# A split-precision MLP: one 512-column product under each high part of the weights, and a VectorE add of its two halves

## Chip, cores, metric

One core of one Trainium2 chip. The metric is device time in microseconds (us), the median of several executions.

## What is computed

Two decoder blocks of two layers each, on 256 rows of 1024 columns in float32: latent attention, an MLP, block attention with a relative bias, a second MLP, then a gated delta rule and a second attention. The change touches the two MLPs only. Cut to them, the reference is:

```python
def sq_relu_mlp(h, w_in, w_out):
    a = jax.nn.relu(h @ w_in)
    return (a * a) @ w_out
...
        h = rms_norm(x, mlp_norm[i])
        x = x + sq_relu_mlp(h, mlp_w_in[i], mlp_w_out[i])
```

`w_in` is 1024 x 4096, `w_out` 4096 x 1024, for each of the two layers.

## The kernel before

**Split products.** Every float32 operand is held as two fp32r tiles, a high part (a copy rounded to fp32r, made on ScalarE) and a low part (the rest, a subtraction on VectorE). A product of split operands is three matmuls (`mm3`): high by high, high by low, low by high.

**Weights.** `load_w` moves 128 x 1024 float32 by one DMA of SyncE's queue into a `raw` tile (four buffers), then writes the high part (line 166, ScalarE) and the low part (line 167, VectorE; for f = 0 GpSimd). `w_in` blocks go to tiles `whi` and `wlo` (four buffers each), `w_out` blocks to fixed slots, printed as `s` in the trace.

**The MLP** (`mlp`). `transpose_x` writes the normed rows' transpose `hT`: for each k of 8 a high part and a low part of 128 x 256, in two slots. Then a loop over 16 blocks f of 256 hidden columns:

- the first product: for each half j of 128 hidden columns and each k of 8, `mm3` with the weights as the stationary operand and `hT` as the moving one (256 columns), 48 matmuls into one PSUM tile `p` with both halves side by side (for f = 0 into two tiles);
- Relu out of PSUM into `r` (line 671; line 664 for f = 0), the square `sq` (line 673), its high part `ah` (line 676) and low part `al` (line 677);
- the split of two `w_out` blocks;
- in layer 0 a piece of the bias setup (`extra`): masks on VectorE (line 402), four matmuls (line 418) into two PSUM tiles, two copies on ScalarE (line 420);
- the second product of the block before (`second(f - 1)`), 24 matmuls of 512 columns, with `ah` and `al` as the stationary operand, added up over all f in four PSUM tiles `acc`.

PSUM has four `acc` and four `aux` buffers; `p`, the tiles of line 418 and those of the transposes take `aux`. `r`, `sq`, `ah` and `al` take `w2k` tiles (seven buffers).

**Order.** Each engine takes its own queue in the order written when the kernel is built. A planner makes that order from the program's; it isn't the program's order: in the trace the high part of `w_in` block f + 2 stands ahead of the Relu of f on ScalarE.

Of the kernel before, what the change touches and what calls it, by code (L numbers as in the profile page):

```python
# [11 lines left out]
F32R = mybir.dt.float32r  # L12
I32 = mybir.dt.int32
AF = mybir.ActivationFunctionType
ALU = mybir.AluOpType
# [4 lines left out]
P = 128  # L20
S = 256
NT = 2
D = 1024
KD = D // P
# [86 lines left out]
def kernel(ctx: ExitStack, tc: tile.TileContext, I: dict, out: bass.AP, small_at: dict):  # L111
    nc = tc.nc
    V, A, G, T = nc.vector, nc.scalar, nc.gpsimd, nc.tensor
# [10 lines left out]
    def slot(i, shape, dt=F32):  # L124

        return big.tile(shape, dt, tag=f"s{i}", name=f"s{i}")

    def w2k(shape, dt=F32):
        return wk.tile(shape, dt, tag="w2k", name="w2k", bufs=7)
# [4 lines left out]
    def acc_tile():  # L134
        return ps.tile([P, 512], F32, tag="acc", name="acc")

    def aux_tile():
        return ps.tile([P, 512], F32, tag="aux", name="aux")
# [34 lines left out]
    def mm3(o, l, r, start, stop):  # L173
        T.matmul(o, lhsT=l[0], rhs=r[0], start=start, stop=False)  # L174
        T.matmul(o, lhsT=l[0], rhs=r[1], start=False, stop=False)  # L175
        T.matmul(o, lhsT=l[1], rhs=r[0], start=False, stop=stop)  # L176

    def sl(pair, *idx):
        return (pair[0][idx], pair[1][idx])
# [32 lines left out]
    ident, cmask = C["ident"], C["cmask"]  # L212
    xT0 = slot(10, [P, KD, S])
    x = cp.tile([P, NT, D], F32, tag="x", name="x")

    def gain(name, k=0):
        return C[name][:, k:k + 1]
# [24 lines left out]
    def ms_eps(src, name, after=None):  # L242

        ss = st.tile([P, NT, 2], F32, tag="ss", name="ss")
        with queued(after):
            for t in range(NT):
                mean_sq(ss, src, t)
        e = st.tile([P, NT], F32, tag="mse" + name, name="mse")
        V.tensor_tensor(e, ss[:, :, 0], ss[:, :, 1], op=ALU.add)
        V.tensor_scalar(e, e, 1.0 / D, EPS, op0=ALU.mult, op1=ALU.add)  # L250
        return e

    def evac_split(hi, lo, p, g=None):

        if g is None:
            i = A.activation(hi, p, AF.Copy)
            j = V.tensor_tensor(lo, p, hi.bitcast(F32), op=ALU.subtract)
        else:
            i = A.activation(hi, p, AF.Copy, scale=g)  # L259
            j = V.scalar_tensor_tensor(lo, p, g, hi.bitcast(F32), op0=ALU.mult, op1=ALU.subtract)  # L260
        return i.ins, j.ins

    def pair_tile(i, n):
        return slot(i, [P, n, S], F32R), slot(i + 1, [P, n, S], F32R)

    def transpose_x(src, gnames, slots):

        outs = [pair_tile(tg, KD) for tg in slots]
        for k2 in range(KD // 2):
            p = aux_tile()  # L270
            for j in range(2):
                k = 2 * k2 + j
                for t in range(NT):
                    T.transpose(p[:, j * 256 + t * P:j * 256 + (t + 1) * P], src[:, t, k * P:(k + 1) * P], ident)
            for j in range(2):
                k = 2 * k2 + j
                for (hi, lo), (gn, off) in zip(outs, gnames):
                    last = evac_split(hi[:, k], lo[:, k], p[:, j * 256:(j + 1) * 256], gain(gn, off + k))
        return outs, last

    def wview(name, l=None):
        w = I[name] if l is None else I[name][l]
        return w.rearrange("(k p) n -> p k n", p=P)
# [349 lines left out]


    def mlp(l, extra=None):
        (hT,), last = transpose_x(x, [("mlp_norm", 8 * l)], [1])
        r2 = st.tile([P, NT], F32, tag="r2", name="r2")
        w1 = wview("mlp_w_in", l)
        w2 = wview("mlp_w_out", l)
        ya = [[acc_tile() for _ in range(2)] for _ in range(NT)]  # L640
        NF = DFF // 256
        pend = []

        def second(f, aa, wc):
            for kk in range(2):
                for hf in range(2):
                    for t in range(NT):
                        mm3(ya[t][hf], sl(aa, slice(None), kk, slice(t * P, (t + 1) * P)),
                            sl(wc[kk], slice(None), slice(hf * 512, (hf + 1) * 512)),
                            f == 0 and kk == 0, f == NF - 1 and kk == 1)  # L650

        for f in range(NF):
            wc = load_w(w1[:, :, f * 256:(f + 1) * 256], KD, 256, (G,) if f == 0 else None, after=last if f == 1 else None)
            r = w2k([P, 512])
            if f == 0:

                pj = [aux_tile() for _ in range(2)]
                for k4 in range(2):
                    for j in range(2):
                        for k in range(4 * k4, 4 * k4 + 4):  # L660
                            mm3(pj[j][:, 0:S], sl(wc[k], slice(None), slice(j * P, (j + 1) * P)), sl(hT, slice(None), k),
                                k == 0, k == KD - 1)
                for j in range(2):
                    A.activation(r[:, j * S:(j + 1) * S], pj[j][:, 0:S], AF.Relu)
            else:
                p = aux_tile()
                for j in range(2):
                    for k in range(KD):
                        mm3(p[:, j * S:(j + 1) * S], sl(wc[k], slice(None), slice(j * P, (j + 1) * P)),
                            sl(hT, slice(None), k), k == 0, k == KD - 1)  # L670
                A.activation(r, p, AF.Relu)
            sq = w2k([P, 512])
            V.tensor_tensor(sq, r, r, op=ALU.mult)
            ah = w2k([P, 2, S], F32R)
            al = w2k([P, 2, S], F32R)
            A.activation(ah.rearrange("p a b -> p (a b)"), sq, AF.Copy)  # L676
            V.tensor_tensor(al.rearrange("p a b -> p (a b)"), sq, ah.rearrange("p a b -> p (a b)").bitcast(F32),  # L677
                            op=ALU.subtract)
            wo = load_w(w2[:, 2 * f:2 * f + 2, :], 2, D, (G,) if f == 0 else None,
                        [slot(i, [P, 2048], F32R) for i in ((5, 6), (7, 11))[f % 2]],  # L680
                        last if f == 0 else None)
            pend.append((f, (ah, al), wo))
            if f == 3:
                V.reciprocal(r2, ms_eps(x, "m", last))
            if extra is not None:
                extra(f)
            if len(pend) > 1:
                second(*pend.pop(0))
        second(*pend.pop(0))
        for hf in range(2):  # L690
            for t in range(NT):
                xs = x[:, t, hf * 512:(hf + 1) * 512]
                V.scalar_tensor_tensor(xs, ya[t][hf], r2[:, t:t + 1], xs, op0=ALU.mult, op1=ALU.add)
# [626 lines left out]
```

## Time and profile before

| | us |
|---|---|
| median of 3 runs (lowest, highest) | 964.49 (960.13, 966.01) |
| profiled execution | 965.93 |
| its span, first to last instruction | 964.1 |

| engine | busy us | share of the span |
|---|---|---|
| TensorE, matmuls | 905.0 | 94% |
| TensorE, weight loads | 789.9 | 82% |
| VectorE | 635.4 | 66% |
| ScalarE | 522.7 | 54% |
| GpSimd | 151.1 | 16% |

Weight loads overlap matmuls, and the ends of matmuls are modelled: for what a matmul costs in a stream, take the distance from one start to the next, not its duration. PE is TensorE's matmuls, PEld its weight loads, DVE VectorE, ACT ScalarE, POOL GpSimd, SP SyncE; SPq is SyncE's queue, where loads are issued. A wait names the instruction that released it.

### The profile page before, as it was taken

The numbers are of one execution on the slowest core, as the hardware profiler recorded it, in microseconds if no ns is written. First come the engines' busy times: TensorE is split into PE (matmuls) and PEld (weight loads), VectorE is DVE, ScalarE is ACT, GpSimd is POOL, SyncE is SP. The second block draws the span as 40 slices with busy tenths as digits, with TensorE's granted clock in tenths as the row PEclk, the third lists the DMA queues.
The fourth block names the chain that finished last, engine by engine and source line by source line (L and its number), as shares of the span: only waits on it lengthen the run. The fifth ranks groups of instructions, "written<-read, shape, count | busy, mean of one in ns | idle before, by whom it ended". The sixth has DMA issues, their size and how long they took to land. (4 is left out here: it accounts for less than half of the span.)

```text
span 964.1 us, 14699 instructions
## 1 busy us (share of the span) xinstructions
PE 905.0 (94%) x5474; PEld 789.9 (82%) x5474; DVE 635.4 (66%) x1335; ACT 522.7 (54%) x967; POOL 151.1 (16%) x194
## 2 busy tenths in 40 slices
PE   8799889999999999999999999998995998998995
PEld 8676589989998878778999999888994986887784
DVE  6897376655556666757554555678983688757775
ACT  6576354644556556646534454478653136754652
POOL 1421122222222300022000000010387000000000
PEclk9799999999999999999999999999997999999998
DMA  8345247677767864436666566354843115445431
GB/s 292 115 146 186 66 131 220 192 198 214 205 197 209 166 196 151 154 109 198 196 195 198 175 195 183 105 166 140 215 149 98 45 41 181 135 170 174 133 109 67
DMA packets 97304, 154.62 MB, mean 160 GB/s; under 512 B 10840, under 2 KB 65920, under 8 KB 96976
## 3 DMA queue, kind: packets, MB, share of 16 engines
q1 hardware_dynamic: 87072, 141.53, 46.9%
q0 software_dynamic: 10016, 12.11, 6.0%
q8 instruction: 43, 0.70, 0.3%
q14 instruction: 29, 0.24, 0.1%
q10 hardware_dynamic: 144, 0.03, 0.0%
HBM read 147.84 MB, written 5.78 MB: 159 GB/s over the span
## 5 line engine op out<-in xcount | busy, mean ns | idle before, releaser
L167 DVE TENSOR_TENSOR wlo<-raw,whi 128x1024 fp32r<-128x1024 f32 (+3 forms) x194 | 236.7, 1223 | 201.9 <-ACT whi L166 200.6
L166 ACT ACTIVATE whi<-raw 128x1024 fp32r<-128x1024 f32 (+3 forms) x202 | 206.0, 1025 | 217.0 <-DMA raw<-in_mlp_w_in_dram 137.6
L174 PE MATMUL acc<-whi,s 128*128 128x512 f32 (+2 forms) x408 | 162.1, 401 | 3.5 <-ACT whi L166 2.6
L175 PE MATMUL acc<-wlo,s 128*128 128x512 f32 (+2 forms) x408 | 160.4, 394 | 0.5 <-DVE wlo L167 0.5
L176 PE MATMUL acc<-whi,s 128*128 128x512 f32 (+2 forms) x408 | 158.9, 391 | 0.0
L176 PE MATMUL aux<-s,wlo 128*128 128x256 f32 (+2 forms) x528 | 149.5, 283 | 3.1 <-DVE wlo L167 3.1
L174 PE MATMUL aux<-s,whi 128*128 128x256 f32 (+2 forms) x528 | 149.4, 283 | 2.3 <-DVE s L260 2.3
L175 PE MATMUL aux<-s,whi 128*128 128x256 f32 (+2 forms) x528 | 149.3, 283 | 0.0
L174 PEld LDWEIGHTS aux<-s,whi 128*128 128x128 f32 (+2 forms) x528 | 99.6, 189 | 4.6 <-DVE s L260 2.8
L176 PEld LDWEIGHTS aux<-s,wlo 128*128 128x128 f32 (+2 forms) x528 | 99.6, 189 | 3.9 <-DVE wlo L167 3.6
L174 PE MATMUL acc<-s,w2k 128*128 128x512 f32 x256 | 100.1, 391 | 1.7 <-ACT w2k L676 1.7
L176 PE MATMUL acc<-s,w2k 128*128 128x512 f32 x256 | 100.2, 391 | 1.1 <-DVE w2k L677 1.1
L175 PEld LDWEIGHTS aux<-s,whi 128*128 128x128 f32 (+2 forms) x528 | 99.6, 189 | 1.6
L175 PE MATMUL acc<-s,w2k 128*128 128x512 f32 x256 | 100.0, 391 | 0.0
L174 PEld LDWEIGHTS acc<-whi,s 128*128 128x128 f32 x408 | 77.6, 191 | 20.6 <-ACT whi L166 3.1
L176 PEld LDWEIGHTS acc<-whi,s 128*128 128x128 f32 x408 | 78.6, 193 | 14.0 <-DVE s L1278 0.3
L175 PEld LDWEIGHTS acc<-wlo,s 128*128 128x128 f32 x408 | 78.2, 192 | 13.2 <-DVE wlo L167 1.3
L167 DVE TENSOR_TENSOR s<-raw,s 128x1024 fp32r<-128x1024 f32 x64 | 75.7, 1219 | 5.3 <-ACT s L166 5.3
L176 PE MATMUL acc<-s,wlo 128*128 128x256 f32 x256 | 73.4, 288 | 6.2 <-DVE wlo L167 6.2
L175 PE MATMUL acc<-s,whi 128*128 128x256 f32 x256 | 73.7, 288 | 0.5 <-DVE s L260 0.2
L174 PE MATMUL acc<-s,whi 128*128 128x256 f32 x256 | 73.7, 288 | 0.4 <-ACT s L259 0.2
L166 ACT ACTIVATE s<-raw 128x1024 fp32r<-128x1024 f32 x68 | 68.3, 1048 | 7.2 <-DMA raw<-in_mlp_w_out_dram 6.0
(357 smaller groups left out, 1486.2 us busy)
## 6 DMA issues: line engine op xcount, KB each, us to landing
raw<-in_mlp_w_in_dram SPq DMA_DIRECT2D x64, 512.0 KB, 5.3
raw<-in_mlp_w_out_dram SPq DMA_DIRECT2D x64, 512.0 KB, 3.9
raw<-in_gdn_w_in_dram SPq DMA_DIRECT2D x32, 512.0 KB, 4.4
raw<-in_moba_w_qkv_dram SPq DMA_DIRECT2D x24, 512.0 KB, 4.4
raw<-in_fox_w_in_dram SPq DMA_DIRECT2D x16, 512.0 KB, 4.9
raw<-in_kv_w_dram SPq DMA_DIRECT2D x16, 512.0 KB, 3.9
raw<-in_mla_w_o_dram SPq DMA_DIRECT2D x8, 512.0 KB, 3.9
bias_d<-s POOLq DMA_DIRECT2D x64, 64.0 KB, 4.5
```

Of the source, the lines that this page charges most:

```text
L166: i = A.activation(hi[:, :k * b], rs, AF.Copy)
L167: j = e.tensor_tensor(lo[:, :k * b], rs, hi[:, :k * b].bitcast(F32), op=ALU.subtract)
L174: T.matmul(o, lhsT=l[0], rhs=r[0], start=start, stop=False)
L175: T.matmul(o, lhsT=l[0], rhs=r[1], start=False, stop=False)
L176: T.matmul(o, lhsT=l[1], rhs=r[0], start=False, stop=stop)
```

## The change

`transpose_x2` stores `hT` so that for each k the high and the low part stand next to each other, 512 contiguous columns. The first product of a block then uses, for each j and k, two matmuls in place of three: the high part of the weights by all 512 columns, and the low part of the weights by the 256 high columns, added into the left half. Each half j has a PSUM tile of its own. The left half of it holds high by high and low by high, the right half high by low. Evacuation per half j: ScalarE copies the right half to `r`, VectorE adds the left half to it. Relu and square become one scalar_tensor_tensor, max(r, 0) * r. `al` and `ah` are as before, and so is the second product.

```diff
--- before.py
+++ after.py
@@ -277,6 +277,21 @@
                 for (hi, lo), (gn, off) in zip(outs, gnames):
                     last = evac_split(hi[:, k], lo[:, k], p[:, j * 256:(j + 1) * 256], gain(gn, off + k))
         return outs, last
+
+    def transpose_x2(src, gn, off, slots):
+
+        outs = [slot(i, [P, KD // 2, 2, S], F32R) for i in slots]
+        hT = [outs[k // 4][:, k % 4] for k in range(KD)]
+        for k2 in range(KD // 2):
+            p = aux_tile()
+            for j in range(2):
+                k = 2 * k2 + j
+                for t in range(NT):
+                    T.transpose(p[:, j * 256 + t * P:j * 256 + (t + 1) * P], src[:, t, k * P:(k + 1) * P], ident)
+            for j in range(2):
+                k = 2 * k2 + j
+                last = evac_split(hT[k][:, 0], hT[k][:, 1], p[:, j * 256:(j + 1) * 256], gain(gn, off + k))
+        return hT, last
 
     def wview(name, l=None):
         w = I[name] if l is None else I[name][l]
@@ -633,7 +648,7 @@
 
 
     def mlp(l, extra=None):
-        (hT,), last = transpose_x(x, [("mlp_norm", 8 * l)], [1])
+        hT, last = transpose_x2(x, "mlp_norm", 8 * l, (1, 2))
         r2 = st.tile([P, NT], F32, tag="r2", name="r2")
         w1 = wview("mlp_w_in", l)
         w2 = wview("mlp_w_out", l)
@@ -651,26 +666,29 @@
 
         for f in range(NF):
             wc = load_w(w1[:, :, f * 256:(f + 1) * 256], KD, 256, (G,) if f == 0 else None, after=last if f == 1 else None)
-            r = w2k([P, 512])
+
+            pj = [aux_tile() for _ in range(2)]
+
+            def first(j, ks):
+                for k in ks:
+                    w = sl(wc[k], slice(None), slice(j * P, (j + 1) * P))
+                    T.matmul(pj[j], lhsT=w[0], rhs=hT[k].rearrange("p a b -> p (a b)"), start=k == 0, stop=False)
+                    T.matmul(pj[j][:, 0:S], lhsT=w[1], rhs=hT[k][:, 0], start=False, stop=k == KD - 1)
+
             if f == 0:
 
-                pj = [aux_tile() for _ in range(2)]
                 for k4 in range(2):
                     for j in range(2):
-                        for k in range(4 * k4, 4 * k4 + 4):
-                            mm3(pj[j][:, 0:S], sl(wc[k], slice(None), slice(j * P, (j + 1) * P)), sl(hT, slice(None), k),
-                                k == 0, k == KD - 1)
+                        first(j, range(4 * k4, 4 * k4 + 4))
+            else:
                 for j in range(2):
-                    A.activation(r[:, j * S:(j + 1) * S], pj[j][:, 0:S], AF.Relu)
-            else:
-                p = aux_tile()
-                for j in range(2):
-                    for k in range(KD):
-                        mm3(p[:, j * S:(j + 1) * S], sl(wc[k], slice(None), slice(j * P, (j + 1) * P)),
-                            sl(hT, slice(None), k), k == 0, k == KD - 1)
-                A.activation(r, p, AF.Relu)
+                    first(j, range(KD))
+            r = w2k([P, 512])
+            for j in range(2):
+                A.activation(r[:, j * S:(j + 1) * S], pj[j][:, S:2 * S], AF.Copy)
+                V.tensor_tensor(r[:, j * S:(j + 1) * S], pj[j][:, 0:S], r[:, j * S:(j + 1) * S], op=ALU.add)
             sq = w2k([P, 512])
-            V.tensor_tensor(sq, r, r, op=ALU.mult)
+            V.scalar_tensor_tensor(sq, r, 0.0, r, op0=ALU.max, op1=ALU.mult)
             ah = w2k([P, 2, S], F32R)
             al = w2k([P, 2, S], F32R)
             A.activation(ah.rearrange("p a b -> p (a b)"), sq, AF.Copy)
```

## Rows read from the trace of the kernel before

**Rows 1.** Windows, both MLP layers: us, busy us (instructions), PEclk, DMA share, GB/s

```profile
125.80:311.50 185.70, 182.95 (x1192) 166.94 (x1192) 113.17 (x157) 99.75 (x140) 47.71 (x58) 1.00 0.70 200
432.40:613.80 181.40, 179.87 (x1153) 164.30 (x1154) 100.29 (x106) 86.00 (x110) 5.75 (x2) 1.00 0.61 191
```

**Rows 2.** Waits in 430 to 446: who<-for whom: us, times, longest

```profile
PE aux L176 <- DVE wlo L167: 1.5, 1, 1.5
```

**Rows 3.** Waits in 140 to 306, the first layer's steady part

```profile
PE acc L176 <- DVE w2k L677: 1.1, 2, 0.6
```

**Rows 4.** Waits in 446 to 602, the second layer's steady part

```profile
ACT whi L166 <- DMA raw<-in_mlp_w_in_dram: 67.6, 19, 6.3
```

**Rows 5.** Timeline, one turn: start us, us, engine, line, out<-in, form [idle <-releaser]

```profile
518.16 1.06 ACT L166 ACTIVATE whi<-raw 128x1024 fp32r<-128x1024 f32 x1 [5.42 <-DMA raw<-in_mlp_w_in_dram]
519.13 0.58 ACT L671 ACTIVATE w2k<-aux 128x512 f32<-128x512 f32 x1
519.26 1.23 DVE L167 TENSOR_TENSOR wlo<-raw,whi 128x1024 fp32r<-128x1024 f32 x1 [4.95 <-ACT whi L166]
520.40 0.68 DVE L673 TENSOR_TENSOR w2k<-w2k 128x512 f32<-128x512 f32 x1
522.14 0.69 DVE L677 TENSOR_TENSOR w2k<-w2k 128x512 fp32r<-128x512 f32 x1
522.74 2.36 DVE L167 TENSOR_TENSOR s<-raw,s 128x1024 fp32r<-128x1024 f32 x2
523.99 1.51 SPq L163 DMA_DIRECT2D raw<-in_mlp_w_in_dram  x2
```

**Rows 6.** Second layer: two turns eight apart, then the `al` of f = 13

```profile
496.84 1.06 ACT L166 ACTIVATE whi<-raw 128x1024 fp32r<-128x1024 f32 x1 [6.33 <-DMA raw<-in_mlp_w_in_dram]
...
584.74 1.06 ACT L166 ACTIVATE whi<-raw 128x1024 fp32r<-128x1024 f32 x1 [5.95 <-DMA raw<-in_mlp_w_in_dram]
...
588.72 0.69 DVE L677 TENSOR_TENSOR w2k<-w2k 128x512 fp32r<-128x512 f32 x1
...
592.12 0.39 PE L176 MATMUL acc<-s,w2k 128*128 128x512 f32 x1
```

**Rows 7.** Timeline of TensorE: starts of second, first and again second product

```profile
513.11 0.40 PE L174 MATMUL acc<-s,w2k 128*128 128x512 f32 x1
...
518.58 0.28 PE L174 MATMUL aux<-s,whi 128*128 128x256 f32 x1
...
524.33 0.40 PE L174 MATMUL acc<-s,w2k 128*128 128x512 f32 x1
```

**Rows 8.** First layer: starts of two turns, and of two matmuls reading `al`

```profile
194.54 1.06 ACT L166 ACTIVATE whi<-raw 128x1024 fp32r<-128x1024 f32 x1 [5.82 <-DMA raw<-in_mlp_w_in_dram]
...
288.43 1.06 ACT L166 ACTIVATE whi<-raw 128x1024 fp32r<-128x1024 f32 x1 [5.12 <-DMA raw<-in_mlp_w_in_dram]
...
271.32 0.40 PE L176 MATMUL acc<-s,w2k 128*128 128x512 f32 x1
...
306.46 0.40 PE L176 MATMUL acc<-s,w2k 128*128 128x512 f32 x1
```

**Rows 9.** Groups by line and form: busy us, mean ns | idle before, releaser

```profile
L1276 DVE TENSOR_TENSOR w1k<-aux,s 128x256 f32<-128x256 f32 x8 | 3.4, 424 | 5.6 <-PE aux L362 5.3
L260 DVE SCALAR_TENSOR_TENSOR s<-aux,gains,s 128x256 fp32r<-128x256 f32 x45 | 19.2, 478 | 7.8 <-ACT s L259 7.5
L664 ACT ACTIVATE w2k<-aux 128x256 f32<-128x256 f32 x4 | 1.5, 376 | 0.9 <-PE aux L176 0.8
```

**Rows 10.** Timeline, first layer, one turn on ScalarE and VectorE

```profile
264.67 1.06 ACT L166 ACTIVATE whi<-raw 128x1024 fp32r<-128x1024 f32 x1 [5.37 <-DMA raw<-in_mlp_w_in_dram]
265.63 0.58 ACT L671 ACTIVATE w2k<-aux 128x512 f32<-128x512 f32 x1
266.11 1.06 ACT L420 ACTIVATE s<-aux 64x512 f32<-64x512 f32 x2
...
268.14 1.22 DVE L167 TENSOR_TENSOR wlo<-raw,whi 128x1024 fp32r<-128x1024 f32 x1 [0.56 <-ACT whi L166]
```

## Prediction

> **What bounds the kernel now.** First I read the busy time in two stretches [rows 1]: the two MLP layers, 185.7 and 181.4 us of the span, and in both TensorE's matmuls are busy for nearly all of it, at a granted clock of 1.00, the upper level (2.4 GHz). VectorE is busy for 113.2 and 100.3 us of them, ScalarE for 99.8 and 86.0. So I asked whether TensorE ever waits there. Two kinds of wait show: at the second column block (f = 1), 1.5 us for low parts of weights in the second layer [rows 2], with its like in the first; and, in the steady part of the first layer, two waits of 1.1 us together for `al`, the last step of the chain that evacuates a product [rows 3]. The steady part of the second layer has none.
>
> That last wait tells what runs close behind TensorE. The sum of waits of the second layer's steady part [rows 4] has ScalarE waiting 67.6 us for the `raw` tiles of `w_in`. The timeline of one turn shows the loop [rows 5]: the high part of a landed `w_in` block starts on ScalarE at 518.16; VectorE then works almost without a pause through its low part, the square, the second low part, `al`, and the low part of a `w_out` block (522.74). The end of that one frees a `raw` tile, SyncE issues the next `w_in` load (523.99), and ScalarE idles until it lands, 5.42 us before this turn. Nothing in this loop waits for TensorE. Its turn took (584.74 - 496.84)/8 = 10.99 us, over the eight turns between [rows 6]; TensorE's took 524.33 - 513.11 = 11.22 [rows 7]. The slack is thin: the `al` of f = 13 ended at 588.72 + 0.69 = 589.41, and the matmul that reads it began at 592.12 [rows 6], 2.7 us later, gathered at 0.23 a turn. In the first layer the loop took (288.43 - 194.54)/8 = 11.74 and TensorE, over three blocks, (306.46 - 271.32)/3 = 11.71 [rows 8]: level.
>
> So TensorE bounds, and a second bound lies within 2% of it. Both change.
>
> **The change: products.** The first product of a column block had 48 matmuls of 256 columns in 518.58 to 524.33, 0.1198 us each; the second product 24 of 512 in 513.11 to 518.58, 0.2279 each [rows 7]. Three of 256 (0.3594) become one of 512 and one of 256 (0.3477): 0.0117 less, 16 times a block, 0.187 a block, 32 blocks: **-6.0 us** if nothing else binds. The bounds are nothing (if a 256 behind a 512 is slower than among its like) and these 6.0.
>
> The Trainium skill speaks against even this: its page "TensorE: Matmul & The Clock Gate", section "Back-to-back issue gap", gives an isolated matmul columns/2.4 + 2.5 ns, so joining two would save 2.5 ns and the layers 1.3 us. The rows above give 11.7 ns; I take the rows, since both shapes were measured in this loop.
>
> The gain of f = 0 and of part of f = 1 goes into the wait at f = 1 [rows 2]: the low parts there come no earlier. That leaves about 14 blocks a layer.
>
> **The change: evacuation.** Before, one Relu of 128x512 and one multiply. After, for each half j a Copy of 256 columns (ScalarE), an add of 256 columns with one operand in PSUM (VectorE), then one scalar_tensor_tensor in place of the multiply. Prices [rows 9]: the add 0.424 by its nearest kin (one operand in PSUM, one in SBUF, same size), the Copy 0.376. In a row VectorE overlaps by 0.09 (519.26 + 1.23 against 520.40 [rows 5]), so an add takes 0.34. For scalar_tensor_tensor against tensor_tensor at one size: 0.478 against 0.424 [rows 9], so +0.05. In all about 0.73 us of VectorE a block, which idles 4.95 us a turn waiting for a load [rows 5]: hidden, unless it lands between the first low part and the `w_out` low part, where it lengthens the loop one for one.
>
> Where it lands depends on the order in which each engine takes its queue, fixed when the kernel is built. The Relu now stands behind the high part of the first `w_in` block (519.13, after 518.16 [rows 5]). That fits an order made by when things become ready: this block's tile is freed by the last product to use it (j = 1, k = 3), a quarter of 5.75 us before the product ends, and the Relu can go when it ends. By that logic the copy of half j = 0, ready at mid product, goes ahead of this high part, into the idle time, and its add too; the copy of half j = 1 stays where the Relu is, with the second high part queued behind it. So I charge **one add and the dearer square, 0.34 + 0.05 = 0.39 a turn**; bounds 0 and 0.73.
>
> *Second layer.* By f = 13 ten such turns have passed (the nine of rows 6 with its own, and one before): `al` at 589.41 + 3.9 = 593.3, where the matmul needed it at 592.12 before: 1.2 us later, and the last product gives back 0.2. So **+1.0**, not -2.7: TensorE would stand still at `al` by some tenths a turn.
>
> *First layer.* Here the turn runs another way [rows 10]: VectorE idles 0.56 before the second low part, since ScalarE first does the Relu and two copies (1.06 together). The 0.39 fits into that idle time. A 256 Copy in the Relu's place takes 0.28 (0.376 less the 0.10 by which the Relu's 0.58 overlaps: 266.11 - 265.63 = 0.48), so the turn becomes 11.74 - 0.20 = 11.54, and TensorE's 11.71 - 0.19 = 11.52: 0.18 gained for some nine turns, **-1.6**. Against it: four `aux` buffers, of which a block now takes two and the bias step (L418) two more, so the second half of the next block needs the buffer that the second add frees. That add ends 2.66 us after the turn's start (high part 1.10, low part 1.14, add 0.42). From there the half takes 8 x 0.348 = 2.78, the bias step 4 x 0.12 = 0.48, and two matmuls of 512 run before the one that reads `al`, 0.46: 6.38 after the turn's start, 271.05 for the turn of 264.67, against 271.32 now [rows 8, 10]. It is just in time; in turns with a late load it is not. I charge **+0.6**, between 0 and 1.3.
>
> The rest costs nothing: `transpose_x2` does the same 16 transposes and 16 evacuations in another layout; the first product waits for the low part of `hT` as before. No DMA is added, and the queues of SyncE and GpSimd stay as they are. The tile `r` is held longer, from the first copy to the square, but six of the seven `w2k` buffers suffice for it, `sq` and two pairs of `ah` and `al`.
>
> Sum: +1.0 - 1.6 + 0.6 = **0**. Own time 965.93 (span 964.1 and 1.8 around it) stays; it stands 1.4 above the median of runs, 964.49, so I forecast 964.5.
>
> **Rivals.**
> 1. *The loop has room (faster).* Both adds run while ScalarE waits for a load, or loads land earlier; TensorE bounds throughout: 28 blocks by 0.187 = -5.2: 959.3. For: 4.95 us of idle time a turn. Against: the second half is ready last, and its add feeds the square inside the chain.
> 2. *Both halves behind the load (slower).* If the copy of j = 0 is queued after the first high part, 0.73 joins the turn. Second layer: 589.41 + 7.3 = 596.7, +4.6. First: 0.73 less the 0.56, +0.17 a turn for nine turns 1.5; and the next block's first half waits for the first add: 2.66 + 5.56 + 0.48 + 0.46 = 9.2 after the turn's start, 273.8 against 271.3, +2.5 once. In all +8.6: 973.1. It decides as soon as the copy of j = 0 starts after the high part of the next `w_in` block. For: the Relu stands there today. Against: j = 0 is ready half a product earlier.
> 3. *Joining saves nothing.* If a 512 costs two of 256 where it stands among them, a block gains nothing. The second layer is still set by the loop, +1.2; the first gains nothing: 965.7. Against: both shapes measured in the same loop [rows 7]. The Trainium skill's formula on the page named above gives 0.04 a block, which would be 965.3.
> 4. *Another order altogether*, as loads taken in another sequence: unpriced, either side.
>
> **Numbers.** Chances: mine 0.50, first rival 0.17, second 0.20, third 0.05, fourth 0.08. Mine by itself lies within 961 to 968 (the bounds 0 to 1.3 of the buffer wait, 0.05 of the square, loads that vary). The range, 958 to 975, takes in the first two rivals and leaves out the fourth. About 1% (9.6 us) is what this kernel's measurement can tell from no change. Even the full 6.0 us is not faster by that: 0.05 for it, by the fourth. Slower by 1% (above 974.1): half of the second and part of the fourth, 0.15. The rest 0.80.
>
> **What would show it.** Products: 512 and 256 alternating at 0.348 a pair, and 5.56 a block. Order: on ScalarE the copy of j = 0 ahead of the first high part, of j = 1 behind it. Second layer: TensorE's turn at 11.3 or so instead of 11.03, with waits at L176 for `al`; turns of the loop at 11.4. First layer: no longer waits than 1 us at `al`, and short ones for an `aux` buffer. Wrong if no such waits show (rival 1) or if a pair takes 0.359 (rival 3).

## The result, and the profile after

| | before | after |
|---|---|---|
| median, us | 967.42 (960.13 to 970.88) | 960.54 (955.41 to 965.93) |
| profiled execution, us | 965.93 | 956.22 |
| its span, us | 964.1 | 954.4 |

The ratio is 0.9924, 95% interval 0.9908 to 0.9941: the change saves 0.6 to 0.9%. The time lies inside the stated range of 958 to 975, but the forecast itself, no change at 964.5, was wrong, and so were most of the reasons for it.

The page after, the line of the engines (busy us, share of the span, instructions):

```profile
PE 899.1 (94%) x4962; PEld 761.1 (80%) x4962; DVE 659.1 (69%) x1399; ACT 528.6 (55%) x997; POOL 152.5 (16%) x194
```

VectorE does 24 us more than before, as charged (0.73 a block), and ScalarE 6 more; TensorE waits once for this added work in the two layers, 0.4 us for an add. The windows of the two layers, from the first matmul of the first product to the last of the second (columns as in [rows 1]):

```profile
126.17:313.22 187.05, 185.56 (x960) 158.06 (x961) 127.58 (x194) 103.99 (x157) 53.41 (x66) 1.00 0.72 208
426.46:606.20 179.74, 178.11 (x896) 150.53 (x897) 113.33 (x138) 88.72 (x125) 5.74 (x2) 1.00 0.61 193
```

Cut by the same two matmuls, the layers of before take 193.41 and 181.36 us. So the first gained 6.36 (forecast: 1.0) and the second 1.6 (forecast: lost 1.0); between the layers lie 113.24 us in both kernels. What remains of the 9.7 us between the two spans stands ahead of the layers (+0.4) and behind them (-2.1); the tail varied between 348.0 and 350.8 over the runs below with no edit in it, so it is no gain of the change.

The waits of TensorE for weights and for the adds in the two layers (who <- for whom: us, times, longest), first layer first. The waits for `al` of [rows 3] have no counterpart; there is no wait for `ah` either.

```profile
...
PE aux L676 <- DVE wlo L167: 1.1, 1, 1.1
PE aux L675 <- DVE w2k L689: 0.4, 1, 0.4
...
PE aux L676 <- DVE wlo L167: 1.6, 1, 1.6
```

The timeline of one turn in the second layer, answering to [rows 5]; ScalarE, then VectorE, then SyncE's queue. L688 is the copy, L689 the add, L691 the square, L694 `ah`, L695 `al`.

```profile
489.09 1.06 ACT L166 ACTIVATE whi<-raw 128x1024 fp32r<-128x1024 f32 x1 [4.29 <-DMA raw<-in_mlp_w_in_dram]
499.52 1.06 ACT L166 ACTIVATE whi<-raw 128x1024 fp32r<-128x1024 f32 x1 [3.61 <-DMA raw<-in_mlp_w_in_dram]
509.97 1.06 ACT L166 ACTIVATE whi<-raw 128x1024 fp32r<-128x1024 f32 x1 [2.95 <-DMA raw<-in_mlp_w_in_dram]
510.94 0.62 ACT L694 ACTIVATE w2k<-w2k 128x512 fp32r<-128x512 f32 x1
511.46 1.04 ACT L166 ACTIVATE whi<-raw 128x1024 fp32r<-128x1024 f32 x1
512.41 1.99 ACT L166 ACTIVATE s<-raw 128x1024 fp32r<-128x1024 f32 x2
514.91 0.38 ACT L688 ACTIVATE w2k<-aux 128x256 f32<-128x256 f32 x1 [0.51 <-PE aux L676]
517.74 0.38 ACT L688 ACTIVATE w2k<-aux 128x256 f32<-128x256 f32 x1 [2.45 <-PE aux L676]
520.70 1.06 ACT L166 ACTIVATE whi<-raw 128x1024 fp32r<-128x1024 f32 x1 [2.58 <-DMA raw<-in_mlp_w_in_dram]
...
511.06 1.23 DVE L167 TENSOR_TENSOR wlo<-raw,whi 128x1024 fp32r<-128x1024 f32 x1 [2.86 <-ACT whi L166]
512.21 0.69 DVE L695 TENSOR_TENSOR w2k<-w2k 128x512 fp32r<-128x512 f32 x1
...
513.94 2.35 DVE L167 TENSOR_TENSOR s<-raw,s 128x1024 fp32r<-128x1024 f32 x2
516.21 0.42 DVE L689 TENSOR_TENSOR w2k<-aux,w2k 128x256 f32<-128x256 f32 x1
518.16 0.42 DVE L689 TENSOR_TENSOR w2k<-aux,w2k 128x256 f32<-128x256 f32 x1 [1.53 <-ACT w2k L688]
518.62 0.69 DVE L691 SCALAR_TENSOR_TENSOR w2k<-w2k 128x512 f32<-128x512 f32 x1
...
515.19 1.51 SPq L163 DMA_DIRECT2D raw<-in_mlp_w_in_dram  x2
```

Here is what the forecast missed. Before, the Relu and the square stood behind the first high part of the next `w_in` block (519.13 and 520.40 behind 518.16 [rows 5]). After, both copies, both adds *and* the square stand ahead of it, in the time in which the engines wait for the load (514.91 to 520.70). From the start of the high part to the issue of the next `w_in` load took 523.99 - 518.16 = 5.83 before, and takes 515.19 - 509.97 = 5.22 now: 0.61 less, which is the square (0.69 less the 0.09 by which neighbours overlap). The turn fell from 10.99 to 499.52 - 489.09 = 10.43 and 10.45. The forecast had it grow by 0.39. The loop now runs ahead until TensorE holds it: in 446 to 602 ScalarE waits 32.9 us for `w_in` instead of 67.6 [rows 4], and 26.2 for TensorE instead, at the copies.

```profile
ACT whi L166 <- DMA raw<-in_mlp_w_in_dram: 32.9, 17, 4.6
ACT w2k L688 <- PE aux L676: 26.2, 19, 2.4
```

TensorE in the second layer, answering to [rows 7]: a first product from 500.79, its second product from 506.43, the next first product.

```profile
500.79 0.39 PE L675 MATMUL aux<-s,whi 128*128 128x512 f32 x1
...
506.43 0.40 PE L174 MATMUL acc<-s,w2k 128*128 128x512 f32 x1
...
511.90 0.39 PE L675 MATMUL aux<-s,whi 128*128 128x512 f32 x1
```

The block takes 5.64 (before 5.75), a pair 5.64/16 = 0.3525 against the forecast 0.3477. TensorE's turn is 511.90 - 500.79 = 11.11 against 11.22; 16 of them and the wait at f = 1 make nearly the whole layer.

### The profile page after: what moved, and what is told of

It is laid out like the page before. It is cut to its first block, busy times and chain, and to the rows that moved or that the text cites. A ratio compares the mean times of both kernels' runs of the same rounds, so it can differ in the third digit from the quotient of the medians.

```text
span 954.4 us, 13772 instructions
## 1 busy us (share of the span) xinstructions
PE 899.1 (94%) x4962; PEld 761.1 (80%) x4962; DVE 659.1 (69%) x1399; ACT 528.6 (55%) x997; POOL 152.5 (16%) x194
## 5 line engine op out<-in xcount | busy, mean ns | idle before, releaser
L675 PE MATMUL aux<-s,whi 128*128 128x512 f32 x512 | 182.3, 399 | 2.7 <-DVE s L260 2.3
L676 PE MATMUL aux<-s,wlo 128*128 128x256 f32 x512 | 143.9, 281 | 2.7 <-DVE wlo L167 2.7
L675 PEld LDWEIGHTS aux<-s,whi 128*128 128x128 f32 x512 | 96.2, 188 | 26.7 <-DVE s L260 2.8
L676 PEld LDWEIGHTS aux<-s,wlo 128*128 128x128 f32 x512 | 96.7, 189 | 4.5 <-DVE wlo L167 3.4
L167 DVE TENSOR_TENSOR s<-raw,s 128x1024 fp32r<-128x1024 f32 x64 | 75.7, 1219 | 11.6 <-ACT s L166 11.4
L441 POOL DMA_DIRECT2D bias_d<-s x64 | 48.3, 986 | 130.7 <-ACT s L435 112.4
L176 PEld LDWEIGHTS acc<-s,w2k 128*128 128x128 f32 x256 | 48.1, 188 | 10.3
```

The lines of the kernel that those rows point to most:

```text
L167: j = e.tensor_tensor(lo[:, :k * b], rs, hi[:, :k * b].bitcast(F32), op=ALU.subtract)
L441: nc.gpsimd.dma_start(bias_d[q0:q0 + 8].rearrange("g h k -> h g k"), stg[r0:r0 + 8], accum_op=ALU.add if part else ALU.bypass)
L675: T.matmul(pj[j], lhsT=w[0], rhs=hT[k].rearrange("p a b -> p (a b)"), start=k == 0, stop=False)
L676: T.matmul(pj[j][:, 0:S], lhsT=w[1], rhs=hT[k][:, 0], start=False, stop=k == KD - 1)
```

## Experiments

Two parts of the change came together: two matmuls for three, and another order of the queues, which nobody wrote by hand. The theories: the **order** took the evacuation out of the loop, or the **products** made the gain. Orders are written in letters: W a `w_in` split, O a `w_out` split, R Relu, C copy, + add, Q square, h `ah`, l `al`. A turn of the second layer in the kernel before is OO W R W h on ScalarE and OO W Q W l on VectorE; after, OO CC W h W and OO ++Q W l W.

Medians against before on the same chip, and the stages of the profiled execution (us):

| kernel | median | ratio, 95% interval | first layer | second layer | span |
|---|---|---|---|---|---|
| before | 967.4 to 969.4 | 1 | 193.41 | 181.36 | 964.1 |
| after | 960.54 | 0.9924 (0.9908, 0.9941) | 187.05 | 179.74 | 954.4 |
| three_matmuls | 974.46 | 1.0056 (1.0031, 1.0082) | 197.90 | 189.05 | 976.8 |
| order_alone | 960.5 | 0.9900 (0.9865, 0.9935) | 189.36 | 181.37 | 960.3 |
| three_matmuls_early | 961.88 | 0.9929 (0.9902, 0.9956) | 192.64 | 181.06 | 961.0 |
| before_longer_loop | 976.27 | 1.0066 (1.0029, 1.0102) | 202.17 | 183.78 | 976.4 |
| after_longer_loop | 966.27 | 0.9966 (0.9946, 0.9986) | 192.42 | 180.76 | 960.8 |
| joined_late | 962.14 | 0.9930 (0.9895, 0.9964) | 186.68 | 178.15 | 960.1 |
| joined_late_in_order | 957.99 | 0.9879 (0.9838, 0.9920) | 187.99 | 179.74 | 958.2 |
| before_load_ahead | 961.16 | 0.9915 (0.9882, 0.9948) | 189.37 | 181.37 | 959.2 |
| halves_high_first | 958.37 | 0.9898 (0.9852, 0.9945) | 188.49 | 177.97 | 954.3 |
| high_first | 958.12 | 0.9895 (0.9862, 0.9929) | 186.76 | 177.59 | 954.3 |
| high_first_tail | 954.0 | 0.9845 (0.9815, 0.9875) | 186.52 | 177.00 | 954.5 |

Differences of 2 us are not told apart by the medians; the stages tell more, since a layer that TensorE bounds repeats within 0.1 (181.36, 181.37, 181.37 in three kernels). But each stage is read from one execution, and that of the changed kernel lies 4.3 us below its median. Four of the first layers (three_matmuls, three_matmuls_early and both longer loops) hold a stretch at a lower granted clock, which cost each some 1.6 us (shown in the last section); all other layers of the table ran at 1.00.

### The new evacuation without the joined products: three_matmuls

```diff
-T.matmul(pj[j], lhsT=w[0], rhs=hT[k].rearrange("p a b -> p (a b)"), start=k == 0, stop=False)
+if k == 0:
+    T.matmul(pj[j], lhsT=w[0], rhs=hT[k].rearrange("p a b -> p (a b)"), start=True, stop=False)
+else:
+    T.matmul(pj[j][:, 0:S], lhsT=w[0], rhs=hT[k][:, 0], start=False, stop=False)
+    T.matmul(pj[j][:, S:2 * S], lhsT=w[0], rhs=hT[k][:, 1], start=False, stop=False)
```

> The changed kernel with its old products: per j and k three matmuls of 256 columns again (for k = 0 the joined one, as it opens the PSUM tile), 46 a block instead of 32; storage and evacuation in halves as in the changed kernel. The planner then puts the copy of j = 0 ahead of the high part of the next w_in block and the copy of j = 1 and its add behind it, the very order that the prediction assumed. Order theory (the gain comes from the evacuation leaving the loop of loads): TensorE's turn 11.2 in the second layer, the loop's 11.4 (0.39 more than before's 10.99), so waits for al of 1 to 2 us in all and a second layer of 182 to 183 us against before's 181.4 and the changed kernel's 179.7; first layer 190 to 193. Total -2 to +2 us against before. Rival (halves help by themselves, whatever the order): no waits for al, second layer 181.3, first 189.5, total -4. Products theory (all of the gain is the joined matmul): total as before, both layers as before (193.4 and 181.4).

Measured: 0.6% slower than before, layers 4.5 (1.6 of it by the clock) and 7.7 us longer. The order theory had the direction right and the size wrong (a second layer of 182 to 183 expected, 189.05 measured). With 46 matmuls a block, all but two of them of 256, the planner writes OO C W C W h and OO + W + W Q l, the very order that the prediction assumed for the changed kernel. So the order that came with the change hangs on the shape of the products. One turn in the second layer, SyncE's issue last:

```profile
516.43 1.06 ACT L166 ACTIVATE whi<-raw 128x1024 fp32r<-128x1024 f32 x1 [3.84 <-DMA raw<-in_mlp_w_in_dram]
528.38 1.06 ACT L166 ACTIVATE whi<-raw 128x1024 fp32r<-128x1024 f32 x1 [3.87 <-DMA raw<-in_mlp_w_in_dram]
...
519.86 1.23 DVE L167 TENSOR_TENSOR wlo<-raw,whi 128x1024 fp32r<-128x1024 f32 x1 [0.77 <-ACT whi L166]
521.00 0.68 DVE L695 SCALAR_TENSOR_TENSOR w2k<-w2k 128x512 f32<-128x512 f32 x1
522.38 0.69 DVE L699 TENSOR_TENSOR w2k<-w2k 128x512 fp32r<-128x512 f32 x1 [0.70 <-ACT w2k L698]
523.33 2.36 DVE L167 TENSOR_TENSOR s<-raw,s 128x1024 fp32r<-128x1024 f32 x2 [0.25 <-ACT s L166]
...
524.58 1.51 SPq L163 DMA_DIRECT2D raw<-in_mlp_w_in_dram  x2
```

The turn takes 528.38 - 516.43 = 11.95, against 10.99: +0.96, where the prediction priced this order at +0.39. It had counted the add, and not that the square now falls behind the second low part, so that VectorE waits 0.70 for ScalarE to make `ah` and 0.25 more for the high part of `w_out`, nor that it waits 0.77 for the second high part. From high part to issue it is 8.15, 2.32 more than before; 1.36 of it comes back because the load then needs only 528.38 - 524.58 = 3.80 to the next high part, against 10.99 - 5.83 = 5.16.

### The order without the joined products: order_alone

The kernel before, with the splits of `w_in` block f queued behind Relu and square of block f - 2 (OO R W h W and OO Q W l W):

```diff
+        behind = {}
...
-            wc = load_w(w1[:, :, f * 256:(f + 1) * 256], KD, 256, (G,) if f == 0 else None, after=last if f == 1 else None)
+            wc = load_w(w1[:, :, f * 256:(f + 1) * 256], KD, 256, (G,) if f == 0 else None,
+                        after=last if f == 1 else behind.get(f - 2))
...
+            behind[f] = (i.ins, j.ins)
```

> The kernel before, with one thing changed: the splits of the w_in block of f are queued behind the Relu and the square of block f - 2 on ScalarE and VectorE. Products, layout and evacuation as before. Order theory: the second layer had no waits, so it stays at 181.4; in the first the waits for al and ah (3.9 us of lost time by the starts of its blocks) go, 193.4 becomes 189.5; total -3 to -4 us, a ratio of 0.996 to 0.997. Products theory: order does nothing, total within 1 us of before.

Measured: first layer 189.36, second 181.37, both to 0.2 of what the order theory said; no wait for `ah` or `al` is left. The median, 1.0% below before, can't be told from that of the changed kernel; it lies 8.2 us below before where 3 to 4 were expected (the profiled spans differ by 3.8), and where the rest lies is not shown. The turn, with the Relu (L673) and the square (L675) in the wait for the load:

```profile
492.15 1.06 ACT L166 ACTIVATE whi<-raw 128x1024 fp32r<-128x1024 f32 x1 [4.84 <-DMA raw<-in_mlp_w_in_dram]
497.87 0.60 ACT L673 ACTIVATE w2k<-aux 128x512 f32<-128x512 f32 x1 [1.30 <-PE aux L176]
502.69 1.06 ACT L166 ACTIVATE whi<-raw 128x1024 fp32r<-128x1024 f32 x1 [4.21 <-DMA raw<-in_mlp_w_in_dram]
...
498.50 0.69 DVE L675 TENSOR_TENSOR w2k<-w2k 128x512 f32<-128x512 f32 x1
...
497.37 1.52 SPq L163 DMA_DIRECT2D raw<-in_mlp_w_in_dram  x2
```

502.69 - 492.15 = 10.54, and 5.22 from high part to issue, as in the changed kernel. So of the 8.0 us by which the layers shrank, 4.05 come from the order, all in the first layer: 1.75 in the two turns with waits for `al`, where the loop was level with TensorE (second products of 6.27 and 6.46 us before, 5.49 now), and 2.3 at the last block, where before had a wait of 1.69 for `ah` (its lines stand further down, with high_first_tail). The second layer, which had slack, gains nothing by it.

### The products under the new order: three_matmuls_early

three_matmuls with the same device (splits of block f behind the last copy and the square of f - 2).

```diff
...
+                i = A.activation(r[:, j * S:(j + 1) * S], pj[j][:, S:2 * S], AF.Copy)
...
+            q = V.scalar_tensor_tensor(sq, r, 0.0, r, op0=ALU.max, op1=ALU.mult)
+            behind[f] = (i.ins, q.ins)
```

> Three matmuls of 256 for each j and k (46 a block), evacuation in halves as in the changed kernel, and the w_in splits of a block queued behind the copies and the square of the block two before, so that in the second layer both engines take copies, adds and square ahead of the next high part. If the order decides: as order_alone, second layer 181.0 to 181.4 us and first 189 to 190, no waits for ah or al in the second layer, a block's product 5.75; 961 to 963. If the joined products decide: as three_matmuls, 189 and 198, 974.

Measured: the second layer falls from 189.05 to 181.06 by the order alone. What the joined products then add is the step to the changed kernel, 181.06 - 179.74 = 1.3 us, and from order_alone 1.6: about 15 blocks by 0.11 (three_matmuls_early joins two of its 46, and its block takes 5.73). The first layer missed its forecast by 3 us: a wait of 1.83 for `ah` at the last block is back there, with low parts for the next part of the program queued ahead of the second add (see high_first_tail), and behind that wait comes the stretch at the lower clock, 1.6 more.

### How much room the loop has: before_longer_loop and after_longer_loop

`al` is written twice, so that each turn has 0.60 us more of VectorE between the high part and the load's issue.

```diff
+            V.tensor_tensor(al.rearrange("p a b -> p (a b)"), sq, ah.rearrange("p a b -> p (a b)").bitcast(F32),
+                            op=ALU.subtract)
```

> The kernel before with the subtraction that writes al done twice, 0.60 us more of VectorE in every block, inside the loop of loads (between the second low part and the w_out low part). If the loop is the second bound close behind TensorE: second layer's turn of the loop 11.6 against TensorE's 11.22, ten turns of 0.6 less the slack of 2.7 at f = 13: +3.3, to 184.7; first layer, level already, +0.6 for some twelve turns: +7, to 200. Total +10 us, ratio 1.010. If TensorE alone bounds: nothing, as VectorE idles 5 us a turn.

> The changed kernel with al written twice, the same 0.60 us. Its loop turned in 10.45 in the second layer when nothing held it, against TensorE's 11.11: with 0.6 it stays at 11.05, under TensorE. Order theory: second layer 179.7 to 180.5, first layer 187 to 189 (its loop has 0.3 to 1 us a turn to spare there), total 0 to +2 us against the changed kernel, so still faster than before by 5. If the changed kernel's loop has no room: +8 us or more, slower than before.

Measured: +8.8 and +2.4 us in the layers of before, +5.4 and +1.0 in those of after. Waits of TensorE for `ah` and `al` in the first layer, up to 322 us: before_longer_loop (`al` alone), then after_longer_loop:

```profile
PE acc L176 <- DVE w2k L679: 5.7, 9, 1.1
```

```profile
PE acc L174 <- ACT w2k L694: 1.4, 1, 1.4
PE acc L176 <- DVE w2k L697: 1.4, 2, 0.7
```

The loop was a second bound in the first layer, as the prediction said, and the change moved it away from TensorE. Eight of the nine waits in before_longer_loop lie in the loop's turns, from 203 to 315 us. None of the three in after_longer_loop does: they stand at f = 1 (141.29) and at the last block (309.85 and 311.30), and between these TensorE waits for nothing. So the new loop takes 0.60 a turn without holding TensorE, and the +5.4 lies at the ends of the layer, 1.0 at f = 1 and 4.4 at the last block, 1.6 of it by the lower clock, which is in the +8.8 as well. The expectation for after_longer_loop (first layer 187 to 189, 0 to +2 us in all) missed that, as it priced the turns alone. In the second layers no turn waits in either kernel: the +2.4 lies at the same two places, the +1.0 at f = 1.

### Evacuation behind the high part after all: joined_late, joined_late_in_order, before_load_ahead

The changed kernel, with the load of `w_in` block f + 2 written ahead of the `w_out` load of f, and copies and adds queued behind its first split (OO W C W C h and OO W + W + Q l). Shown is the edit of joined_late_in_order. In joined_late blocks 1 and 2 of `w_in` were taken in each other's place; the work per block is the same.

```diff
...
+            for n in (2, 3) if f == 1 else (f + 2,) if 1 < f < NF - 2 else ():
+                wcs.append(load_w(w1[:, :, n * 256:(n + 1) * 256], KD, 256))
+                ahead = first_split[0]
             for j in range(2):
+                with queued(ahead):
                     A.activation(r[:, j * S:(j + 1) * S], pj[j][:, S:2 * S], AF.Copy)
...
```

> The changed kernel's products and evacuation, but with the copies and adds of a block queued behind the first high and low part of the next w_in block (ScalarE W C W C h, VectorE W + W + Q l in nearly every turn of the second layer), as the Relu and square stood in the kernel before. If the order of the queues decides: the turn of the loop lengthens as in three_matmuls (11.9 us there), so the second layer takes 187 to 189 us and the first 194 to 198, with waits at the matmul that reads al, although a pair still costs 0.3525; the kernel is slower than before, 971 to 976. If the joined products decide: the layers stay as in the changed kernel, 179.7 and 187, and the time is 960.

Measured: the expectation fell. With almost the order of three_matmuls the kernel was not slower but 0.7% faster than before. "Behind the high part" was the wrong name for the cause. In this kernel ScalarE waits for `w_out` loads, not for `w_in`: a `w_in` tile lies landed when its split comes up, and copies, adds, square, `ah` and `al` run between the `w_in` splits and the `w_out` splits, in *that* wait. So I put a second form of the theory: the evacuation is free wherever it lies in the wait for the load that closes the loop. Two runs on it, one in the right order of blocks, one on the kernel before with the load written ahead and no order forced:

> joined_late with the blocks in their order (there blocks 1 and 2 of w_in were exchanged), the load of block f + 2 written ahead of the w_out load of f from f = 1 on. joined_late did not become slower, though copies and adds stood behind the first high part: there ScalarE waited for w_out loads instead, and copies, adds, square, ah and al ran between the w_in splits and the w_out splits, while a w_out load was under way. If the place of the evacuation against the load that is waited for decides: turns of 10.2 to 10.4 us until TensorE binds, no waits for ah or al in the second layer's steady part, second layer 178 to 180, first 186 to 188.5, waits of ScalarE for raw<-in_mlp_w_out. If the gain of joined_late came from the exchanged blocks: turns of 11.9, second layer 187 or more.

> The kernel before with one edit: from f = 1 on the load of w_in block f + 2 is written ahead of the w_out load of f, so that a w_in tile lies landed when its split comes up and the load that ScalarE waits for is that of w_out. Relu still stands behind the high parts of the next w_in block on ScalarE. If evacuation is free wherever it lies in the wait for a load: as order_alone, first layer 189 to 190 with no waits for al in its steady part, second layer 181 to 181.5, a turn of the loop in the first ones no longer than 10.5. If a Relu behind the high part is bad by itself: the first layer stays at 193, with waits for al. What stands ahead of the layers may change by up to 4 us, as in joined_late (130.17 instead of 125.77 before the first product).

Measured: joined_late_in_order has the second layer of the changed kernel, 179.74, and a first of 187.99; before_load_ahead has 189.37 and 181.37, the layers of order_alone, though the Relu stands behind both high parts. Its turn in the second layer (L677 Relu, L684 `ah`):

```profile
487.14 2.00 ACT L167 ACTIVATE whi<-raw 128x1024 fp32r<-128x1024 f32 x2
489.03 0.58 ACT L677 ACTIVATE w2k<-aux 128x512 f32<-128x512 f32 x1
491.40 0.63 ACT L684 ACTIVATE w2k<-w2k 128x512 fp32r<-128x512 f32 x1 [1.79 <-DVE w2k L681]
494.89 1.06 ACT L167 ACTIVATE s<-raw 128x1024 fp32r<-128x1024 f32 x1 [2.86 <-DMA raw<-in_mlp_w_out_dram]
497.19 1.04 ACT L167 ACTIVATE whi<-raw 128x1024 fp32r<-128x1024 f32 x1
```

From one pair of high parts to the next, 497.19 - 487.14 = 10.05, with Relu, square, `ah` and `al` all between the end of the high parts at 489.14 and the `w_out` split at 494.89. So the second form holds for both product shapes. In these three runs the place of the load moved together with that of the evacuation; copies queued behind the first split with the loads left as in the changed kernel were not run.

### The pair's price: halves_high_first, high_first, high_first_tail

halves_high_first does, for each half j, the eight matmuls of 512 and then the eight of 256; high_first (f >= 1) the sixteen of 512 of both halves and then the sixteen of 256.

```diff
...
-                    first(j, range(KD))
+                    for z in range(2):
+                        first(j, range(KD), z)
```

Here `first` with z = 0 issues the matmuls of 512 alone, with z = 1 those of 256.

> The changed kernel, but for each half j the eight matmuls of 512 first and then the eight of 256; the order of the other engines' queues is the same. A pair cost 0.3525 us with 512 and 256 in turn, where the distances of each shape in a row give 0.3477. If going back and forth costs the difference: a block takes 5.56 instead of 5.64, the second layer 178.5 to 179.0 and the first 185.9 to 186.5, 2 us less than the changed kernel in all. If the cost lies in the shapes themselves: 5.64, and no difference.

> The changed kernel, but for f >= 1 all sixteen matmuls of 512 of both halves first and then the sixteen of 256. As in halves_high_first a block takes 5.56 if going back and forth costs. Besides, the low parts of the weights are wanted 3.6 us later, so the waits for wlo at f = 1 (1.1 and 1.6 us) go: second layer 177 to 178, first 184.5 to 186, 4 us less than the changed kernel. Against it: both halves are ready only in the last 0.96 us of the product, so copies, adds and square come later; if the loop then lacks time, waits at ah or al appear, and more in the first layer.

Measured, halves_high_first, TensorE's groups of one block in the second layer:

```profile
500.85 1.98 PE L676 MATMUL aux<-s,whi 128*128 128x512 f32 x8
502.67 1.11 PE L678 MATMUL aux<-s,wlo 128*128 128x256 f32 x8
503.62 2.00 PE L676 MATMUL aux<-s,whi 128*128 128x512 f32 x8
505.46 1.11 PE L678 MATMUL aux<-s,wlo 128*128 128x256 f32 x8
506.41 0.40 PE L174 MATMUL acc<-s,w2k 128*128 128x512 f32 x1
```

(506.41 - 500.85)/16 = 0.3475 a pair and 5.56 a block, exactly the sum of the two prices of [rows 7]: the 0.005 a pair was the going back and forth. The second layer is 177.97, a little below its forecast, since its wait for low parts at f = 1 is 0.99 instead of 1.63; with high_first, which also wants the low parts later, 177.59, and its wait for `wlo` at f = 1 is gone. The first layer did not follow: 188.49 and 186.76, since both have a wait for `ah` at the last block (1.67 and 1.35) that the changed kernel hasn't. The kernel before has it too, and I had missed it, because the window of [rows 3] ends at 306. The wait, and ScalarE ahead of it:

```profile
PE acc L174 <- ACT w2k L676: 1.7, 1, 1.7
```

```profile
309.69 1.06 ACT L166 ACTIVATE whi<-raw 128x1024 fp32r<-128x1024 f32 x1 [1.60 <-DMA raw<-in_moba_w_qkv_dram]
310.66 0.58 ACT L671 ACTIVATE w2k<-aux 128x512 f32<-128x512 f32 x1
...
```

The Relu of the last block stands behind a split for the *next* part of the program, which waits for its load. Whether that costs hangs on when the load lands: the same split began at 302.71 in the changed kernel, with no wait behind it, and at 304.10 in halves_high_first. high_first_tail queues those splits behind the last copy and square:

```diff
-            wc = load_w(w[:, 4 * c:4 * c + 4, c0:c0 + n], 4, n)
+            wc = load_w(w[:, 4 * c:4 * c + 4, c0:c0 + n], 4, n, after=list(tail) if c else None)
...
+            tail[:] = [i.ins, q.ins]
```

> high_first, and the two w_qkv splits of the following block attention that stood ahead of the last copy of block 15 in the first layer are queued behind that block's copies and square. In high_first TensorE waited 1.35 us for ah there, in halves_high_first 1.67, in the kernel before 1.69. If the splits ahead are the cause: no such wait, first layer 185 to 185.5, the rest as high_first; 957. If the load is the cause, the wait moves to the first product behind the layer: the stretch between the layers grows from 113.2 by as much.

Measured: the wait for `ah` is gone and the stretch between the layers is 113.23 as before, so the splits ahead were the cause. Two waits for an add stand elsewhere in the first layer (186.52 instead of 185): 0.51 at f = 1, where high_first has 0.41, and a new one of 1.06 at 183.51, whose cause stays open. At 954.0 us, ratio 0.9845 (0.9815 to 0.9875), this is the fastest kernel; its interval lies below that of the changed kernel, though the two were not run side by side.

## Why the prediction failed, and what of it held

**Bounds: held.** TensorE bounds both layers, and in the first the loop is a second bound: lengthening it by 0.60 raised the waits for `al` in the turns of before from two to eight, and brought none into those of the changed kernel. In the second layer the same 0.60 brought none in either.

**Order: the step that failed.** "The copy of half j = 0, ready at mid product, goes ahead of this high part", while "the copy of half j = 1 stays where the Relu is", hence "one add and the dearer square, 0.34 + 0.05 = 0.39 a turn". I took the place of the second half and of the square as given by the old queue. In the new one nothing of the evacuation but `ah` and `al` is left in the path from the high part to the load's issue: -0.61 a turn. Nor does such work lengthen the loop "one for one": 0.60 more took the second layer's turn of before from 10.99 to 11.27 (586.89 - 496.77 over eight turns of before_longer_loop), and 2.32 more in three_matmuls gave 0.96, since the load then landed sooner after its issue. The forecast saw that the added work might be hidden (rival 1), but not that work already there, the square, could move into the same idle time; so rival 1 too gave the layers less, -5.2, than the -8.0 that the trace shows. What rules this is that an engine takes its queue in the order written: the copies wait for nothing once the block's product is done, and whatever stands behind a split waits for that split's load. The Trainium skill, page "PSUM — Partial Sum Buffer", section "Engine vs sequencer instructions", says the same of ScalarE and VectorE ("queues are strict FIFO"); the trace agrees, e.g. in the Relu at 310.66 behind the split that waited 1.60 for its load.

**First layer: -1.6 + 0.6 against -6.36.** The waits for `al` went, as did one of 1.69 for `ah` that stood outside the window I had read. Together 2.8 of recorded waits; order_alone shows that removing them is worth 4.05. The joined products give 1.65 of the rest (15 blocks by 0.11). Some 0.6 is left: from the end of one first product to the start of the next a turn takes 5.92 instead of 5.96, in three_matmuls_early too, and why was not isolated. The wait at f = 1 became 0.55 shorter, but that gives nothing, as forecast: it ends 9.77 us after the layer's first matmul, before 9.78. The wait for an `aux` buffer that I priced at 0.6 is there, 0.4, but at f = 1, where the wait for low parts takes it up.

**Second layer: +1.0 against -1.6.** No wait for `al` arose; TensorE's turn of 11.11 instead of 11.3, and that of the loop 10.44 instead of 11.4.

**Products: right mechanism, wrong size.** A pair costs 0.3525, not 0.3477, so a block saves 0.11 instead of 0.187. I summed two distances measured each among its like, and named a dearer 256 behind a 512 as the bound. The square as scalar_tensor_tensor takes 0.69 against 0.68 for the multiply: the 0.05 for it were not there. The formula of the Trainium skill, page "TensorE: Matmul & The Clock Gate", section "Back-to-back issue gap", which the page gives for an isolated matmul, would have had the joining save 2.5 ns a pair; the runs show 6.9 in turn (0.3594 to 0.3525) and 11.9 in runs of eight.

**Rivals.** The first is what came: both adds run while ScalarE waits for a load, and TensorE bounds throughout. The forecast by itself was 961 to 968; the time lies inside the range only because this rival is in it. That its 959.3 is so close to 960.54 is in part luck: it had the products at 5.2 and nothing for the order, where they gave 3.3 and the order 4.05. The second (both halves behind the load, slower) was run only with the `w_in` load moved ahead, in joined_late and joined_late_in_order, and wasn't slower there. three_matmuls has the order that the prediction assumed for itself, with the old products, and lies 5.7 above before by the medians, so that order too was priced too low. The third fell with the 0.11 a block.

## What to carry to other kernels

When a change alters the shape or number of a planner's instructions, expect the whole order to move, and price the orders rather than the instructions: find the load that closes the loop, sum what each engine does from its landing to the issue of the next, and ask which of it could run during the wait. Two orders that look opposite (evacuation ahead of the split, or behind it) cost about the same here once the evacuation lay in that wait; if the order can be written by hand, that alone may bring most of the gain. Read the waits to the last block of a layer: what follows it is already queued in between.

## What was not expected of the hardware

- **Matmuls of two lengths in turn** cost 0.3525 us a pair of 512 and 256 columns, in runs of eight 0.3475. What makes the 0.005 was not isolated.
- **A stall of TensorE costs more than its recorded wait.** In the first layer of before (starts of three matmuls that otherwise lie 0.228 apart):

```profile
199.00 0.40 PE L175 MATMUL acc<-s,w2k 128*128 128x512 f32 x1
199.91 0.51 PE L176 MATMUL acc<-s,w2k 128*128 128x512 f32 x1 [0.50 <-DVE w2k L677]
200.25 0.40 PE L174 MATMUL acc<-s,w2k 128*128 128x512 f32 x1
```

  From 199.00 to 200.25 they took 1.25 instead of 0.456: 0.79 for a recorded wait of 0.50. Of the difference, 0.17 is only how the wait is recorded (from the modelled end of the matmul before, 0.40 after its start, where the next otherwise starts 0.228 after it); 0.11 lies behind the waiting matmul.
- **A load that is issued earlier need not land as much earlier.** From its issue to the next high part a `w_in` load took 3.80 in three_matmuls, where the `w_out` loads were issued 524.58 - 518.78 = 5.80 ahead of it, and 5.51 in the changed kernel, where they were issued 515.19 - 512.32 = 2.87 ahead. That fits loads sharing the DMA engines, but no run varied the distance alone.
- **The granted clock fell behind some waits at the end of the first layer.** In the last second product of that layer, in the profiled executions of three_matmuls, three_matmuls_early, before_longer_loop and after_longer_loop, the granted clock stood at the lower of its two levels (0.50, 1.2 GHz) for some eight matmuls, which then lay 0.427 apart instead of 0.228: 1.6 us. Shortly before, TensorE had waited there for `ah` (1.81 in three_matmuls, 1.83 in three_matmuls_early, 1.46 and 1.44 in the longer loops). From three_matmuls_early:

```profile
312.15 0.63 PE L174 MATMUL acc<-s,w2k 128*128 128x512 f32 x1
312.58 0.63 PE L175 MATMUL acc<-s,w2k 128*128 128x512 f32 x1
```

  Waits of 1.69, 1.67 and 1.35 at the same place in before, halves_high_first and high_first were followed by no such fall; what decides it stays open.
